# Two-layer sparse-attention trunk on one core: sums moved from GpSimd to VectorE, earlier rotary angles, modulation finished inside the dot products, and a fourth buffer with fewer fp32 blocks in the lead-in

## The chip, the cores and the metric

The kernel runs on one core of a Trainium2 chip. Its engines work side by side, each through its own instruction queue in order: TensorE (PE in the profile; PEld is its weight load), VectorE (DVE), ScalarE (ACT), GpSimd (POOL), and SyncE (SP), which here only issues DMA transfers. Sixteen DMA engines move data between HBM and the on-chip memory. The metric is the device time of one execution in microseconds (us).

## The reference, cut to what matters

Two layers over a sequence of 256 tokens of width 1024, in fp32. Each layer has a mixing and a feed-forward half:

```python
ada = silu(c) @ w_ada[l] + b_ada[l]               # c is one vector; 6 x 1024 results
sh_m, sc_m, g_m, sh_f, sc_f, g_f = split(ada, 6)
h = rms_norm(x, norm_mix[l]) * (1.0 + sc_m) + sh_m
q_a, kc_a, vc_a, ..., g_br = split(h @ w_in[l], ...)  # 4888 columns
y_a = nsa_mixer(...)      # 8 heads of 64: compressed blocks, selected blocks, window
y_b = moba_mixer(...)     # 8 heads of 64
gate_a, gate_b = split(sigmoid(g_br), 2)
x = x + g_m * ((gate_a * (y_a @ w_up_nsa[l]) + gate_b * (y_b @ w_up_moba[l])) @ w_out[l])
h = rms_norm(x, norm_ffn[l]) * (1.0 + sc_f) + sh_f
gt, up = split(h @ w_ffn_in[l], 2)
x = x + g_f * ((silu(gt) * up) @ w_ffn_out[l])
```

Queries and keys are RMS-normalised per head and rotated: `x1*cos - x2*sin`, `x2*cos + x1*sin`, with angles position times 32 inverse frequencies.

## The kernel before

**Who sets the order.** The function `trunk_kernel` describes the work as operations on named values that live in numbered slots of a few arenas. A planner (`Program.order`, `replay` and `rounds`) then decides when the kernel is built in which order every engine issues its operations. It knows one cost for every operation (`_vec`, `act`, `mm` and the figures handed to `raw`), ranks operations by the length of the chain behind them plus a boost, and keeps the best of 60 rounds. Operations allowed on several engines (`engs=("DVE", "POOL")`) are placed by it as well. So a changed cost, slot or engine changes the order of the whole program. For PE there is a constant `STICK`, a bonus for an operation whose array form is that of the one before; it is 0, so unused. A "form" other than `FLAT` is a matmul that uses 64 or fewer rows or columns of the array.

**Dense products.** A weight unit of 128 x 2048 values is loaded into a slot of arena `raw` and split into two fp32r parts by `split_unit`: ACT copies `hi`, DVE subtracts to get `lo`. `mm3` then issues three matmuls per tile (hi*hi, hi*lo, lo*hi). The slot of `raw` is free again when `lo` has been computed. Weights in the tuple `WHOLE` are not split; they are multiplied as plain fp32, and their slot is free only when PE has read it for the last time. An fp32 matmul appears in the profile as two instructions.

**Lead-in (`lead_in`, layer 0).** The normalised x is transposed, and for each of eight blocks k of 128 rows of `w_in` the kernel loads 1 MB of `w_ada` into a slot of `sa` and 1816 columns of `w_in` into a slot of `raw` (three slots; a fourth, 11, only serves values marked spare). Two dot products on DVE (`ada_dot`, one SCALAR_TENSOR_TENSOR of 128x1024 with accumulator each) give shift and scale of the block; `ada_mod` adds the bias and multiplies by the norm's gain in two small DVE operations (`mod_m`); ACT forms the modulated block `hd`, splits it into `hp`, and PE multiplies it into eight PSUM banks. The blocks 0, 2, 4 and 6 are in `WHOLE`.

The table of rotary angles (`angles`) and the products with the gains (`rope_tables`, tiles `ct` and `st`) are computed on POOL; the inverse frequencies come from the array `rows`, loaded after the weights of blocks 0 and 1. The tables of layer 1 are written into the same tiles as soon as layer 0 no longer reads them.

**After the lead-in**, `post_grpA`, `post_qa` and `post_qb` normalise and rotate heads (`rstd_of` does its power -0.5 on POOL; the sums of the two rotated halves may go to DVE or POOL), `mlp` computes the compressed keys and values, and the dense products of the other columns of `w_in`, attention (`nsa`, `moba`), up projections, output projection and feed-forward follow. The remaining `w_ada` rows are streamed through three `aw` tiles and dotted on DVE between other work.

Of the kernel before, what the change touches and what calls it, by code (L numbers as in the profile page):

```python
# [139 lines left out]
class Program:  # L140
# [10 lines left out]
    FLAT, STICK = (P, P), 0.0  # L151
# [417 lines left out]
class Engines:  # L569
# [22 lines left out]
    def tt(self, out, a, b, op, engs=("DVE",)):  # L592
        self._vec(engs, cols(out), True, lambda v: v.tensor_tensor(AP(out), AP(a), AP(b), op=op), [a, b], [out])  # L593
# [9 lines left out]
    def ttr(self, out, a, b, op0, op1, init, accum):  # L603
        self._vec(("DVE",), cols(out), True,
                  lambda v: v.tensor_tensor_reduce(AP(out), AP(a), AP(b), 1.0, init, op0, op1, AP(accum)),  # L605
                  [a, b], [out, accum])
# [114 lines left out]
def trunk_kernel(tc, pools, A):  # L721
# [240 lines left out]
    def rstd_of(ss, n, mul, add, tag):  # L962
# [3 lines left out]
        E_.raw("POOL", 1.1 + 0.13 * n, lambda: nc.gpsimd.tensor_tensor(AP(r), AP(r), AP(mh), op=ALU.pow), [r, mhalf], [r])  # L966
        return r

    def h_rstd(t, log):
# [16 lines left out]
        else:  # L986
            ts(r, s1, 1.0 / D, b, ALU.mult, ALU.add)
            E_.raw("POOL", 1.0, lambda: nc.gpsimd.tensor_tensor(AP(r), AP(r), AP(mhalf), op=ALU.pow), [r, mhalf], [r])
        return xr, r

    def log_soon(late):

        R.boost = 1000.0
        op = R.op({"ACT": (1.28, [lambda: nc.scalar.preload_act_table_set("natural_log_exp_and_others")])}, late, [])
        op.loads = TABLES[3]
        R.boost = 0.0

# [148 lines left out]
    def lead_in(bs, h, W):  # L1146
# [671 lines left out]
```

## Time and profile before

| | us |
|---|---|
| runs shown | 806.29, 2772.15, 805.36 |
| median of them | 806.29 |
| profiled execution, its time | 805.06 |
| span inside the profiled execution | 803.3 |

The profile's page gives busy time per engine, the span in 40 slices, the chain of work that ended last, and groups of instructions by line. Other views are the windows (busy time of each engine in stretches of the span), the timeline (merged instructions in order of time: start, duration, engine, line, operation, and in brackets the idle time before it and what ended it) and the waits. PE's matmuls are pipelined, so a matmul's duration is longer than its distance from the next one; what one costs is read from long unbroken stretches. The TensorE clock was granted in full (9 in every slice, 1.00 in the windows).

### The profile page before, as it was taken

Reading aid. Unit: us, or ns where it says so; the run is one execution under the profiler, and the core shown is the slowest. Engines: PE = TensorE matmul, PEld = TensorE weight load, DVE = VectorE, ACT = ScalarE, POOL = GpSimd, SP = SyncE. Lnnn points to the kernel's source line nnn. Section 1 sums busy time; section 2 is a strip of 40 time slices with the busy share of each in tenths; the row PEclk is TensorE's granted clock in tenths of the full one; section 3 lists DMA queues with packets and bytes.
Section 4 is the critical chain, followed back from the end, with each engine's and each line's share of the span. In section 5 each row is a group of like instructions: output and inputs, shape, how many; then the busy total and the mean of one; then the engine's idle time right before and its main releaser. Section 6 shows DMA issues by size and latency. Waiting matters only on the chain.

```text
span 803.3 us, 10733 instructions
## 1 busy us (share of the span) xinstructions
PE 787.8 (98%) x4062; PEld 623.5 (78%) x4062; DVE 601.1 (75%) x1034; ACT 436.0 (54%) x688; POOL 75.3 (9%) x73
## 2 busy tenths in 40 slices
PE   8998999999999999999999999999999999999997
PEld 4566676778788888888888777677888888888886
DVE  6879999999797878776798799977758435536445
ACT  5445587976373344533585457796538343444432
POOL 3813600001000000000000331000010000000000
PEclk9999999999999999999999999999999999999999
DMA  9967754788758887977774785526573536546631
GB/s 359 415 243 264 253 199 156 239 282 313 267 184 339 317 304 260 337 288 248 301 258 154 271 290 172 191 73 202 198 255 93 170 105 224 191 162 210 209 105 53
DMA packets 74116, 183.85 MB, mean 229 GB/s; under 512 B 4304, under 2 KB 9808, under 8 KB 73552
## 3 DMA queue, kind: packets, MB, share of 16 engines
q1 hardware_dynamic: 73920, 183.08, 64.1%
q8 instruction: 32, 0.52, 0.3%
q14 instruction: 20, 0.16, 0.1%
q10 hardware_dynamic: 144, 0.08, 0.0%
HBM read 182.10 MB, written 1.05 MB: 228 GB/s over the span
## 4 chain that ended last, share of the span: by engine, by line
PE 67%; DVE 5%; ACT 1%; issue 1%; DVEq 0%; ACTq 0%
PE bank L678 61%; PE bank L685 4%; PE bank L659 2%; DVE lo L593 2%; DVE tmp L593 1%; ACT at L642 1%; DVE ss L620 0%; DVE x L593 0%; DVE aw L599 0%; ACT hi L642 0%; DVE at L605 0%; DVE e L593 0%; ACT hp L642 0%; DVE mT L599 0%; DVE tmp L599 0%
## 5 line engine op out<-in xcount | busy, mean ns | idle before, releaser
L678 PE MATMUL bank<-hi,hp 128*128 128x512 f32 (+2 forms) x1344 | 375.6, 383 | 1.6 <-ACT hp L642 0.9
L593 DVE TENSOR_TENSOR lo<-raw,hi 128x2048 fp32r<-128x2048 f32 (+2 forms) x118 | 268.8, 2295 | 121.7 <-ACT hi L642 120.2
L642 ACT ACTIVATE hi<-raw 128x2048 fp32r<-128x2048 f32 (+2 forms) x118 | 221.3, 1893 | 211.8 <-PE bank L678 189.8
L678 PEld LDWEIGHTS bank<-hi,hp 128*128 128x128 f32 x1344 | 243.2, 188 | 56.6 <-issue 6.0
L678 PE MATMUL bank<-lo,hp 128*128 128x512 f32 (+2 forms) x672 | 219.8, 382 | 0.3 <-DVE lo L593 0.3
L678 PEld LDWEIGHTS bank<-lo,hp 128*128 128x128 f32 x672 | 123.8, 188 | 24.8 <-DVE lo L593 2.1
L678 PE MATMUL bank<-hi,aT 128*128 128x512 f32 x352 | 100.4, 394 | 0.3 <-ACT aT L642 0.3
L599 DVE SCALAR_TENSOR_TENSOR aw<-aw,crow 128x1024 f32<-128x1024 f32 x80 | 96.5, 1229 | 4.2 <-DMA aw<-in_w_ada 4.2
L678 PEld LDWEIGHTS bank<-hi,aT 128*128 128x128 f32 x352 | 65.0, 188 | 13.8 <-ACT hi L642 0.6
L678 PE MATMUL bank<-lo,aT 128*128 128x512 f32 x176 | 56.7, 392 | 0.0
L678 PE MATMUL bank<-hi,mT 128*128 128x512 f32 x128 | 40.8, 396 | 0.8 <-DVE mT L599 0.8
L678 PE MATMUL bank<-hi,yy 128*128 128x512 f32 x128 | 40.2, 396 | 0.0
L685 PE MATMUL bank<-ident,tmp 128*128 128x128 f32 x256 | 37.3, 275 | 2.8 <-DVE e L593 0.7
L685 PEld LDWEIGHTS bank<-ident,tmp 128*128 128x128 f32 x256 | 29.9, 140 | 11.5 <-ACT e L651 1.8
L678 PEld LDWEIGHTS bank<-lo,aT 128*128 128x128 f32 x176 | 32.7, 188 | 6.7
L642 ACT ACTIVATE at<-at,nb,rqa 128x128 f32<-128x128 f32 (+1 forms) x64 | 34.1, 535 | 0.7 <-DVE nb L599 0.6
L605 DVE CUSTOM_DVE_ANT_0 at<-bank,maskf 128x128 f32<-128x128 f32 (+1 forms) x96 | 30.6, 351 | 1.6 <-PE bank L685 1.2
L642 ACT ACTIVATE tmp<-bank 128x512 f32<-128x512 f32 (+2 forms) x43 | 20.8, 513 | 18.2 <-PE bank L678 7.2
L593 POOL TENSOR_TENSOR tmp<-tmp,tmp 128x512 f32<-128x512 f32 (+2 forms) x12 | 13.7, 1139 | 176.4 <-DVE tmp L599 158.1
L678 PEld LDWEIGHTS bank<-hi,yy 128*128 128x128 f32 x128 | 24.0, 188 | 6.0 <-issue 0.5
L678 PEld LDWEIGHTS bank<-hi,mT 128*128 128x128 f32 x128 | 23.8, 188 | 6.1 <-DVE mT L599 1.6
L593 DVE TENSOR_TENSOR tmp<-tmp,bank 128x512 f32<-128x512 f32 (+1 forms) x24 | 15.3, 639 | 15.3 <-PE bank L678 14.8
(184 smaller groups left out, 769.9 us busy)
## 6 DMA issues: line engine op xcount, KB each, us to landing
raw<-in_w_ffn_in SPq DMA_DIRECT2D x44, 1024.0 KB, 6.3
aw<-in_w_ada SPq DMA_DIRECT2D x80, 512.0 KB, 5.9
raw<-in_w_in SPq DMA_DIRECT2D x30, 1024.0 KB, 5.2
raw<-in_w_ffn_out SPq DMA_DIRECT2D x22, 1024.0 KB, 5.0
raw<-in_w_out SPq DMA_DIRECT2D x8, 1024.0 KB, 5.1
raw<-in_w_in SPq DMA_DIRECT2D x8, 908.0 KB, 9.2
sa<-in_w_ada SPq DMA_DIRECT2D x7, 1024.0 KB, 12.3
raw<-in_w_up_nsa SPq DMA_DIRECT2D x4, 1024.0 KB, 5.1
```

Of the source, the lines that this page charges most:

```text
L593: self._vec(engs, cols(out), True, lambda v: v.tensor_tensor(AP(out), AP(a), AP(b), op=op), [a, b], [out])
L599: lambda v: v.scalar_tensor_tensor(AP(out), AP(a), AP(s), AP(b), op0=op0, op1=op1, **{k: AP(x) for k, x in kw.items()}),
L605: lambda v: v.tensor_tensor_reduce(AP(out), AP(a), AP(b), 1.0, init, op0, op1, AP(accum)),
L642: op = self.p.op({"ACT": (c, [lambda: self.nc.scalar.activation(AP(out), AP(a), func, **{k: AP(x) for k, x in kw.items()})])}, reads + lis ...
L659: op = self.p.op({"PE": (cost, [lambda: self.nc.tensor.matmul(AP(out), AP(lhsT), AP(rhs), start=start, stop=stop)])}, [lhsT, rhs], [out])
L678: self.nc.tensor.matmul(AP(out), AP(lhsT), AP(rhs), start=first, stop=v.gone == v.terms)
L685: op = self.p.op({"PE": (0.109, [lambda: self.nc.tensor.transpose(AP(out), AP(a), AP(ident))])}, [a, ident], [out])
```

## The change

- **Sums.** The sums of rotated halves, of the queries and of the two gated branches, which could go to DVE or POOL, are DVE only.
- **Angles.** The inverse frequencies move from `rows` to `vecs`, which arrives first. A ScalarE table set with Silu, Sin and Tanh is loaded at the start. Layer 1's `rope_tables` must wait for the gate tile of layer 0's feed-forward.
- **Modulation.** `ada_dot` becomes one `tensor_tensor_reduce` whose scale is a column of the (halved) norm gains and whose start value is a column of the bias prepared by `ada_ready`; `ada_mod` and the bias sums go.
- **Lead-in.** Its raw blocks have an arena of their own, `lraw`, with slots 0, 1, 2 and 17; `WHOLE` is `(0, 3)`.
- **Planner.** `STICK` is 20 and applies after a form that is not `FLAT`, to any other such form; some costs are set anew.

```diff
+SETS = ("exp_and_others", "trig_and_small", "silu_and_others", "natural_log_exp_and_others")
...
-    FLAT, STICK = (P, P), 0.0
+    FLAT, STICK = (P, P), 20.0
...
-                    if e == "PE" and self.STICK:
+                    if e == "PE" and self.STICK and form != self.FLAT:
                         pick = max((c for c in cs if c[0] <= t0 + w), key=lambda c: (
-                            c[1].rank(e) + (self.STICK if c[1].forms and c[1].forms[0] == form else 0.0), -c[1].no))
+                            c[1].rank(e) + (self.STICK if c[1].forms and c[1].forms[0] != self.FLAT else 0.0), -c[1].no))
...
-    def ttr(self, out, a, b, op0, op1, init, accum):
+    def ttr(self, out, a, b, op0, op1, init, accum, scale=1.0):
         self._vec(("DVE",), cols(out), True,
-                  lambda v: v.tensor_tensor_reduce(AP(out), AP(a), AP(b), 1.0, init, op0, op1, AP(accum)),
-                  [a, b], [out, accum])
+                  lambda v: v.tensor_tensor_reduce(AP(out), AP(a), AP(b), AP(scale), AP(init), op0, op1, AP(accum)),
+                  [a, b, init, scale], [out, accum])
...
-WHOLE = (0, 2, 4, 6)
+WHOLE = (0, 3)
...
     arena("raw", (0, 1, 2, 11), (11,))
+    arena("lraw", (0, 1, 2, 17))
...
-    inv = rows.of("inv")[:, :32]
+    inv = vecs.of("inv")[:, NV + 3:NV + 35]
...
-    def ada_dot(w, col):
-        stt(w, w, 0.5, crow, ALU.mult, ALU.mult, accum=col)
-
-    def ada_mod(l, k0, ks, part=None):
-        v = mods[l][k0].of(part)
-        tt(v[:, :, ks], v[:, :, ks], bT[:, l, k0:k0 + 2, ks], ALU.add)
-        tt(v[:, 1, ks], v[:, 1, ks], normT[:, k0 // 3, l, ks], ALU.mult)
+    def ada_dot(w, l, kind, k, col):
+        by = normT[:, kind // 3, l, k:k + 1] if kind in (1, 4) else 0.5
+        ttr(w, w, crow, ALU.mult, ALU.add, bT[:, l, kind, k:k + 1], col, by)
+
+    def ada_ready():
+        ts(normT, normT, 0.5, None, ALU.mult)
+        for a, kind in enumerate((1, 4)):
+            b, nv = bT[:, :, kind], normT[:, a]
+            stt(b, b, 1.0, nv, ALU.add, ALU.mult)
+            ts(b, b, 2.0, None, ALU.mult)
...
-        E_.raw("POOL", 1.1 + 0.13 * n, lambda: nc.gpsimd.tensor_tensor(AP(r), AP(r), AP(mh), op=ALU.pow), [r, mhalf], [r])
+        E_.raw("POOL", 0.5 + 0.22 * n, lambda: nc.gpsimd.tensor_tensor(AP(r), AP(r), AP(mh), op=ALU.pow), [r, mhalf], [r])
...
-            raws[k] = R.val("raw", lambda a: a[:, :NC0])
+            raws[k] = R.val("lraw", lambda a: a[:, :NC0])
...
         dma(vecs, A["vecs"], q="ACT")
+        table_soon(2, [])
...
-        for kind in (1, 4):
-            ts(bT[:, :, kind], bT[:, :, kind], 1.0, None, ALU.add)
+        ada_ready()
...
-                tt(kk.of(br)[:, br * 128:(br + 1) * 128], a, c, ALU.add, engs=("DVE", "POOL"))
+                tt(kk.of(br)[:, br * 128:(br + 1) * 128], a, c, ALU.add)
...
-                    tt(dst, src, pe, ALU.add)
+                    tt(dst, src, pe, ALU.add, extra=0.08)
...
-                    mm(s[:, p * 64:(p + 1) * 64], q[:, p], kbd, False, p == 3)
+                    mm(s[:, p * 64:(p + 1) * 64], q[:, p], kbd, False, p == 3, cost=0.2)
...
-            rope_tables(l, gvec[l])
+            rope_tables(l, gvec[l], [ada[l - 1]["g_f"]])
```

More of the change, by code (lines that the diff above doesn't have):

```diff
@@ L590, in _vec, with tt @@
         self.p.op(alts, reads, writes)
-    def tt(self, out, a, b, op, engs=("DVE",)):
-        self._vec(engs, cols(out), True, lambda v: v.tensor_tensor(AP(out), AP(a), AP(b), op=op), [a, b], [out])
+    def tt(self, out, a, b, op, engs=("DVE",), late=(), extra=0.0):
+        self._vec(engs, cols(out), True, lambda v: v.tensor_tensor(AP(out), AP(a), AP(b), op=op),
+                  [a, b, *late], [out], extra=extra)
     def stt(self, out, a, s, b, op0, op1, accum=None):
@@ L803, in trunk_kernel @@
     NV = 2 * L * KD + L * 6 * KD + L * 16
-    vecs = const("vecs", [P, NV + 3])
-    rows = const("rows", [P, 32 + 256 * L])
+    vecs = const("vecs", [P, NV + 35])
+    rows = const("rows", [P, 256 * L])
     posi = vecs.of("pos")[:, NV:NV + 3].bitcast(I32)
-    inv = rows.of("inv")[:, :32]
-    gvec = [rows.of("g")[:, 32 + 256 * l:32 + 256 * (l + 1)] for l in range(L)]
+    inv = vecs.of("inv")[:, NV + 3:NV + 35]
+    gvec = [rows.of("g")[:, 256 * l:256 * (l + 1)] for l in range(L)]
     normT = vecs.of("norm")[:, :2 * L * KD].rearrange("p (a l k) -> p a l k", a=2, l=L)
@@ L987, in h_rstd, with table_soon @@
             ts(r, s1, 1.0 / D, b, ALU.mult, ALU.add)
-            E_.raw("POOL", 1.0, lambda: nc.gpsimd.tensor_tensor(AP(r), AP(r), AP(mhalf), op=ALU.pow), [r, mhalf], [r])
+            E_.raw("POOL", 0.75, lambda: nc.gpsimd.tensor_tensor(AP(r), AP(r), AP(mhalf), op=ALU.pow), [r, mhalf], [r])
         return xr, r
+    def table_soon(i, late):
+        R.boost = 1000.0
+        op = R.op({"ACT": (1.28, [lambda: nc.scalar.preload_act_table_set(SETS[i])])}, late, [])
+        op.loads = TABLES[i]
+        R.boost = 0.0
     def log_soon(late):
[L993 to L996, printed above, removed]
+        table_soon(3, late)
     def h_norm(t, log=True):
@@ L1067, in rope_tables @@
             tt(ct[:np_].rearrange("p a (h d) -> p (a h) d", h=2), g8,
-               sincos[:np_, 0, t, None, :].to_broadcast([np_, 2 * na, 32]), ALU.mult, engs=("POOL",))
+               sincos[:np_, 0, t, None, :].to_broadcast([np_, 2 * na, 32]), ALU.mult, engs=("POOL",), late=late)
             tt(st[:np_].rearrange("p a (h d) -> p a h d", h=2), gs,
-               nsin[:np_, t, None, :, :].to_broadcast([np_, na, 2, 32]), ALU.mult, engs=("POOL",))
+               nsin[:np_, t, None, :, :].to_broadcast([np_, na, 2, 32]), ALU.mult, engs=("POOL",), late=late)
             CT[t], ST[t] = ct, st
@@ L1303, in post_qa @@
             tt(q.rearrange("p (c g d) -> p g c d", c=4, g=2), a.rearrange("p (g c d) -> p g c d", g=2, c=4),
-               c.rearrange("p (g c d) -> p g c d", g=2, c=4), ALU.add, engs=("DVE", "POOL"))
+               c.rearrange("p (g c d) -> p g c d", g=2, c=4), ALU.add)
             qaT[t] = heads_T(quarter(qv, t, t), q)
@@ L1311, in post_qb @@
             rqb[t] = rstd_of(ss, 8, 1.0, DH * EPS, "rqb")
-            tt(a, a, c, ALU.add, engs=("DVE", "POOL"))
+            tt(a, a, c, ALU.add)
             qbT[t] = heads_T(quarter(qv, 2 + t, 2 + t), a)
@@ L1319, in post_kb @@
             r = rstd_of(ss, 8, 1.0 / DH, EPS, "rkb")
-            tt(a, a, c, ALU.add, engs=("DVE", "POOL"))
+            tt(a, a, c, ALU.add)
             tt(v3(a, DH), v3(a, DH), r[:, :, None].to_broadcast([P, 8, DH]), ALU.mult)
@@ L1411, in mlp @@
             ts(r[:64], ss[:64], 1.0 / DH, EPS, ALU.mult, ALU.add)
-            E_.raw("POOL", 1.2, lambda: nc.gpsimd.tensor_tensor(AP(r)[:64], AP(r)[:64], AP(mhalf)[:64], op=ALU.pow),
+            E_.raw("POOL", 1.5, lambda: nc.gpsimd.tensor_tensor(AP(r)[:64], AP(r)[:64], AP(mhalf)[:64], op=ALU.pow),
                    [r, mhalf], [r])
@@ L1637, in sublayer_mix @@
                 stt(m2, tg[(2 + c, t)], 1.0, bs[("w_up_moba", t)], ALU.add, ALU.mult)
-                tt(m1, m1, m2, ALU.add, engs=("DVE", "POOL"))
+                tt(m1, m1, m2, ALU.add)
                 mT[t] += split_into(quarter(mv[t], 2 * c, c, 0), quarter(mv[t], 2 * c + 1, c, 1), trans4(m1), 0.5)
@@ L1801 @@
                             ("nsa_q_gain", "nsa_k_gain", "moba_q_gain", "moba_k_gain")], axis=1)
-    rows = np.concatenate([np.array(INV_FREQ, np.float32), gains.reshape(-1)])
-    host["vecs"] = np.concatenate([host["vecs"], spots.view(np.float32)], axis=1)
-    host["rows"] = np.repeat(rows[None], P, axis=0)
+    freq = np.repeat(np.array(INV_FREQ, np.float32)[None], P, axis=0)
+    host["vecs"] = np.concatenate([host["vecs"], spots.view(np.float32), freq], axis=1)
+    host["rows"] = np.repeat(gains.reshape(1, -1), P, axis=0)
     arrays, aps = {}, {}
```

9 lines of the change are left out of this document (3 added, 6 removed).

## The prediction

> **What bounds the kernel now.** I read the head of the page, then the windows by stage.
>
> ```profile
> span 803.3 us, 10733 instructions
> PE 787.8 (98%) x4062; PEld 623.5 (78%) x4062; DVE 601.1 (75%) x1034; ACT 436.0 (54%) x688; POOL 75.3 (9%) x73
> ```
>
> ```profile
> 11.74:57.14 45.40, 43.77 (x153) 26.84 (x153) 34.09 (x61) 20.11 (x35) 20.65 (x24) 1.00 0.88 348
> 57.14:70.00 12.86, 9.44 (x103) 7.34 (x104) 12.63 (x30) 6.73 (x15) 2.65 (x2) 1.00 0.61 204
> 70.00:100.00 30.00, 28.28 (x134) 21.37 (x132) 28.45 (x44) 16.22 (x25) 18.46 (x12) 1.00 0.82 285
> 100.00:165.00 65.00, 64.91 (x410) 48.41 (x410) 62.34 (x210) 55.50 (x144) 3.28 (x4) 1.00 0.58 202
> 165.00:440.00 275.00, 273.58 (x1343) 226.30 (x1342) 221.62 (x280) 140.68 (x169) 5.84 (x4) 1.00 0.76 278
> ...
> 790.00:803.30 13.30, 8.65 (x44) 6.61 (x42) 6.53 (x13) 1.75 (x4) 0.00 (x0) 1.00 0.22 80
> ```
>
> The columns are the stretch, its length, busy time of PE, PEld, DVE, ACT and POOL, the granted clock, DMA share and GB/s. PE is the bound: 787.8 of 803.3 us. All its idle time is 15.5 us. So no cover taken off another engine is worth anything except where PE idles: 1.63 us in the lead-in (11.74 to 57.14), 3.42 us behind it (to 70), 1.72 us up to 100, 1.42 us between 165 and 440, and 4.65 us at the end, which this change leaves alone. Everything else must come from fewer PE cycles. Two per cent, about what a measurement of this kernel can tell from no change, is 16 us: more than all the idle time.
>
> **The lead-in: two blocks less in fp32.** Costs of one block are read from the timeline and, for fp32r, from the longest unbroken stretch in the chain.
>
> ```profile
> 23.80 6.27 PE L678 MATMUL bank<-raw,hd 128*128 128x512 f32 x16
> ...
> 231.89 68.46 PE bank L678 x301
> ```
>
> An fp32 block is 16 instructions, 6.27 us. In the chain an fp32r matmul of 512 columns costs 68.46 / 301 = 0.227 us, or 0.444 ns a column. A split block has 3 parts x 2 token tiles x 1816 columns = 10,896 columns: 4.84 us. Two blocks changed from fp32 to split save 2 x 1.43 = 2.9 us; the last fp32 matmul's tail lies inside the 6.27, so I take **2.8 us**, off PE itself. What it adds is two ACT copies and two DVE subtractions:
>
> ```profile
> L593 DVE TENSOR_TENSOR lo<-raw,hi 128x1816 fp32r<-128x1816 f32 x4 | 8.2, 2048 | 3.3 <-ACT hi L642 3.3
> L593 DVE TENSOR_TENSOR mod_m<-mod_m,vecs 128x2 f32<-128x2 f32 (+1 forms) x16 | 3.7, 228 | 0.6
> L593 DVE TENSOR_TENSOR hp<-hd,hp 128x256 fp32r<-128x256 f32 x8 | 4.2, 519 | 2.6 <-ACT hp L642 2.6
> L599 DVE SCALAR_TENSOR_TENSOR aw<-aw,crow 128x1024 f32<-128x1024 f32 x80 | 96.5, 1229 | 4.2 <-DMA aw<-in_w_ada 4.2
> ```
>
> The subtractions cost 2 x 2.05 = 4.1 us, and the sixteen `mod_m` operations that go are worth 3.7. DVE's load in the lead-in stays at about 34.5 of 45.4 us. A split block needs two dots, its `hp` and its `lo`: 2 x 1.23 + 0.52 + 2.05 = 5.03 us of DVE against 4.84 of PE. From block 4 on, with four split blocks in a row, the two run neck and neck; that is a rival below. A block's `hd` follows its dots 2 x 0.23 us sooner.
>
> ```profile
> 18.73 1.56 PE L678 MATMUL bank<-hi,hp 128*128 128x512 f32 x6 [0.63 <-ACT hp L642]
> ...
> 36.23 5.50 PE L678 MATMUL bank<-raw,hd 128*128 128x512 f32 x14 [0.71 <-ACT hd L642]
> ```
>
> These two waits, 1.34 of the stage's 1.63 us, stand behind the dots and `mod_m`; I take **0.4 us** off them, bounds 1.6 gained and 1.5 lost.
>
> **The fourth slot, and what comes after.** The releases explain the loads.
>
> ```profile
> 41.68 0.33 SPq L695 DMA_DIRECT2D raw<-in_w_in  x1
> 46.38 0.33 SPq L695 DMA_DIRECT2D raw<-in_nsa_cmp_k_w  x1
> 46.48 1.72 ACT L642 ACTIVATE hi<-raw 128x1816 fp32r<-128x1816 f32 x1 [0.72 <-DMA raw<-in_w_in]
> ...
> 54.96 1.02 PE L678 MATMUL bank<-raw,hd 128*128 128x512 f32 x2
> 56.01 0.38 SPq L695 DMA_DIRECT2D raw<-in_w_in  x1
> ```
>
> The last raw block was issued at 41.68, when a slot came free, and landed at 46.48. The first weights of the next dense stage were issued at 56.01, just after fp32 block 6 left PE (54.96 + 1.02). With four slots and blocks 4 to 7 split, a slot returns at its subtraction: the lead's queue is never held, and that dense load goes out some 8 us earlier, behind the last lead load and the two `nsa_cmp` loads. What it meets:
>
> ```profile
> 54.93 1.28 ACT L642 ACT_TABLE_LOAD   x1
> 57.78 0.65 PE L685 MATMUL bank<-ident,tmp 128*128 128x128 f32 x4 [0.65 <-ACT e L651]
> 61.95 0.44 PE L685 MATMUL bank<-ident,tmp 128*128 128x128 f32 x2 [0.70 <-DVE e L593]
> 63.70 1.98 PE L659 MATMUL bank<-raw,e 128*31 128x128 f32 x64 [1.26 <-DVE e L593]
> 66.64 2.27 DVE L593 TENSOR_TENSOR lo<-raw,hi 128x2048 fp32r<-128x2048 f32 x1
> ```
>
> PE idles here because only the chain of `post_grpA` feeds it: the first dense unit's `lo` comes at 66.64. Copied and subtracted before 57, it would fill these holes, as soon as the accumulator banks are read out. The early table set also takes the table load (1.28 us) from ACT's path to the first hole. The ScalarE: Activation LUTs page of the Trainium skill (What ACT_TABLE_LOAD costs) puts a switch at about 2.66 us, a load and a drain; here ACT goes on 1.28 us after the load began, so no drain is seen and the sum keeps 1.28. Of 3.42 us idle I take **2.4 us** back; bounds 0 and 3.4. What is late next is DVE, 12.63 of 12.86 busy.
>
> **POOL leaves DVE alone.** Between 70 and 100 DVE is 28.45 of 30 busy, partly because POOL slows it.
>
> ```profile
> 73.92 1.29 POOL L593 TENSOR_TENSOR tmp<-tmp,tmp 128x512 f32<-128x512 f32 x1 [1.60 <-DVE tmp L593]
> 74.36 3.00 DVE L593 TENSOR_TENSOR lo<-raw,hi 128x2048 fp32r<-128x2048 f32 x1
> ...
> 91.54 1.36 DVE L593 TENSOR_TENSOR tmp<-tmp,tmp 32x64 f32<-32x64 f32 x2
> 91.59 0.76 POOL L593 TENSOR_TENSOR st<-rows,nsin 128x256 f32<-128x256 f32 x1 [0.72 <-DVE tmp L593]
> 93.22 0.27 PE L685 MATMUL bank<-ident,kbd_tok 64*128 64x64 f32 x1 [1.41 <-DVE kbd_tok L611]
> ```
>
> The subtraction beside POOL's sum takes 3.00 us, that at 66.64 (quoted above) 2.27: 0.73 lost, and on DVE the sum costs 0.72 (its group, quoted next). So the sum itself is free, and its result is there 0.6 us sooner. The layer-1 tables, which now wait, overlapped the two `tmp` operations (1.36) in the chain for which PE waited 1.41 us. The new wait of the tables holds up POOL's queue only, which the windows show with 3.28 us of work from 100 to 165 and 5.84 from there to 440: little stands behind it. But POOL's power operations stay in the chain of `kbd_tok`. I take **0.5 us** of the 1.72; bounds 1.7 gained, 1.5 lost if the sums only lengthen DVE's queue. The GPSIMD Engine Reference of the Trainium skill (8. Key points) says that POOL shares its memory interfaces with VectorE and that instructions with two on-chip inputs contend; the 3.00 against 2.27 agrees. By the same rule the angles, moved ahead, disturb the dots of the first blocks; that is part of the first rival. The other place where a sum touched PE:
>
> ```profile
> 202.84 1.29 POOL L593 TENSOR_TENSOR tmp<-tmp,tmp 128x512 f32<-128x512 f32 x1 [4.57 <-DVE tmp L599]
> 206.93 0.50 PE L678 MATMUL bank<-hi,mT 128*128 128x512 f32 x1 [0.77 <-DVE mT L599]
> L593 DVE TENSOR_TENSOR tmp<-tmp,tmp 128x512 f32<-128x512 f32 x13 | 9.4, 720 | 0.1
> ```
>
> A DVE sum is 0.72 us instead of 1.29 and spares the subtraction beside it: **0.4 us** of 0.77; bounds 0 and 0.77. The remaining sums lie under a full PE and cost nothing there.
>
> **Early angles.** They ran on POOL deep in the lead-in, behind the load of `rows`.
>
> ```profile
> 7.99 0.74 POOL L988 TENSOR_TENSOR rx<-rx,mhalf 128x1 f32<-128x1 f32 x1 [0.99 <-DVE rx L611]
> ...
> 24.97 1.23 POOL L593 TENSOR_TENSOR tmp<-tmp,tmp 128x96 f32<-128x96 f32 x1
> ```
>
> Now they stand in POOL's queue around the two `rx` (the second is quoted), for which the first transposes wait, and each lasts up to 1.23 us. `ada_ready` adds three small DVE operations before the first dot (0.7 us at the 228 ns of `mod_m`), and the first `mod_m` pair (0.46) goes. Start of block 0: **0.2 us later**; bounds 0.4 earlier and 1.5 later.
>
> **Modulation elsewhere.** The new reduce is seen only on PSUM input with constants.
>
> ```profile
> L605 DVE CUSTOM_DVE_ANT_0 at<-bank,maskf 128x256 f32<-128x256 f32 x48 | 19.0, 417 | 1.4 <-PE bank L685 1.0 <-ACT hi L642 0.5
> L605 DVE CUSTOM_DVE_ANT_0 at<-bank,maskf 128x128 f32<-128x128 f32 x48 | 11.6, 285 | 0.2 <-PE bank L685 0.2
> ```
>
> 128 columns more cost 132 ns, 1.03 ns a column, so 1024 columns take 0.417 + 768 x 0.00103 = 1.21 us against 1.229: nothing. Bounds: 0.1 us less, or half speed, 1.07 us more. **0.**
>
> **Turns of the array.**
>
> ```profile
> 135.05 1.13 PE L659 MATMUL bank<-kk,qq 64*128 64x512 f32 x4
> 136.11 1.09 PE L659 MATMUL bank<-pt,vsw 128*64 128x128 f32 x16
> ```
>
> A burst in another form takes 1.06 us from start to start, where its columns at 0.444 ns (four times 512, two passes each, the two row halves side by side) need 0.91: some 0.15 us a turn. If `STICK` joins two or three bursts: **0.3 us** gained, bounds 1.5 gained (ten joined) and 0.5 lost. The other cost figures only reorder.
>
> **The sum.** 2.8 + 0.4 + 2.4 + 0.5 + 0.4 + 0.3 - 0.2 = 6.6 us. Against the profiled execution: span 803.3 - 6.6 = 796.7, with the 1.8 us around it (805.06 - 803.3) 798.5 us. Of the runs shown the lowest is 805.36 and the median 806.29, so I stay with the profiled execution and keep a microsecond of doubt upward.
>
> **The rivals.**
> - *DVE gives it back* (803.5 us). Six split blocks and the contention of early angles make DVE the clock of the lead-in, the stage behind it, already 98% DVE, gains nothing, and only the saved passes remain, less four blocks at 5.03 instead of 4.84 (0.8) and 0.4 for a later start: 805.06 - 2.8 + 1.2 = 803.5. For: the windows from 57 to 165 show DVE at 95% and more. Against: 11.3 us of DVE idle time in the lead-in. Angles in front of both `rx`, a start 1.5 us late, give 798.5 + 1.3 = 799.8 by themselves, inside the forecast.
> - *The reduce is slower* (814 us, slower than before). If, with two on-chip inputs and column operands, it runs at half speed, each of 16 dots in the lead-in costs 1.07 more: 17 us, of which 11.3 find idle DVE, so 6 remain; and of the 13 between 100 and 165, 14 us, less 2.66 of idle DVE there, 11 remain: 798.5 + 17 = 815, some of it taken up by reordering: 814. It decides from 2.66 / 13 = 0.2 us a dot. For: nothing shows it with column operands. Against: 1.03 ns a column on PSUM.
> - *The plan finds more* (793.4 us): all 6.8 us of idle time from 11.74 to 100 go (3.3 are taken above), the hole at 206 closes (0.4 more) and ten bursts join (1.2 more): 5.1 us under the forecast.
> - *The change doesn't do what it says*, in that the dense load stays behind because the DMA queue, not the slot, held it: then the 2.4 us behind the lead-in are not won, 800.9 us, still in the forecast. Against: 56.01 follows PE's last read at 55.98.
>
> **How the numbers follow.** Forecast, 796 to 801.5: 0.56. DVE gives it back, 801.5 to 805.5: 0.22. More is found, under 796: 0.13. Slower reduce or a worse plan, over 805.5: 0.09. The range reaches into both neighbours: 795 to 804.5. Faster by over 2% means under 790.2, which needs more than all idle time up to 100 beside the passes: 0.02. Slower by over 2%, over 822.4, only if the reduce costs more than half speed: 0.03. The rest, 0.95, is within 2%.
>
> **What would show it.** Right: 32 `raw,hd` matmuls instead of 64; the lead-in's end near 54.5; the first dense `lo` before 57; no table load near 55; no `tmp` sums and, from 70 to 100, no tables on POOL; PE idle from 57 to 70 near 1 us. Wrong: PE waits for `lo` or `hp` in blocks 4 to 7; dots above 1.4 us; new holes of PE after 100, where the plan was full.

## The result, and the profile after

| | before | changed |
|---|---|---|
| median of 8 runs each, us | 806.87 | 801.90 |
| lowest and highest of them | 805.13, 2772.15 (next 809.72) | 800.14, 802.61 |
| profiled execution: time, span | 805.06, 803.3 | 801.24, 799.5 |

The ratio is 0.9938, with a 95% interval of 0.9919 to 0.9956: a small gain, within 2%. The forecast was 798.5 us, with a range of 795 to 804.5.

The head of the changed kernel's page:

```profile
span 799.5 us, 10734 instructions
PE 784.7 (98%) x4077; PEld 626.7 (78%) x4077; DVE 606.7 (76%) x1021; ACT 435.5 (54%) x681; POOL 66.8 (8%) x65
```

and its windows in the stretches used before (columns as there):

```profile
11.74:57.14 45.40, 42.67 (x176) 30.28 (x176) 37.57 (x57) 22.98 (x41) 18.00 (x20) 1.00 0.96 381
57.14:70.00 12.86, 11.45 (x113) 8.99 (x115) 12.70 (x28) 6.52 (x10) 3.04 (x2) 1.00 0.47 170
70.00:100.00 30.00, 27.36 (x136) 21.49 (x135) 27.20 (x54) 15.53 (x28) 14.95 (x6) 1.00 0.76 262
100.00:165.00 65.00, 64.25 (x411) 47.25 (x409) 62.61 (x200) 56.23 (x139) 5.88 (x7) 1.00 0.61 212
165.00:440.00 275.00, 274.15 (x1336) 227.30 (x1335) 225.90 (x276) 139.26 (x167) 1.03 (x1) 1.00 0.76 274
```

PE is busy 3.1 us less (787.8 to 784.7) and idle 0.7 us less (15.5 to 14.8): together the 3.8 us between the spans (the medians lie 5.0 apart; the profiled execution before was one of its faster ones). Idle time of PE by stage is length less busy time:

| stretch | before | changed | difference |
|---|---|---|---|
| 11.74 to 57.14 | 1.63 | 2.73 | +1.10 |
| 57.14 to 70 | 3.42 | 1.41 | -2.01 |
| 70 to 100 | 1.72 | 2.64 | +0.92 |
| 100 to 165 | 0.09 | 0.75 | +0.66 |
| 165 to 440 | 1.42 | 0.85 | -0.57 |

So the time came almost whole from PE's busy time. Behind the lead-in idle time went nearly as forecast; in the lead-in and from 70 to 165 it grew. In these five stretches together it is 0.1 us more, and the 0.7 us less come from the rest of the span. Where it stands, from PE's timeline (start, duration, instruction, and in brackets the idle time before it and who ended it):

```profile
19.18 2.38 PE L680 MATMUL bank<-hi,hp 128*128 128x512 f32 x10 [1.01 <-ACT hi L644]
30.64 5.50 PE L680 MATMUL bank<-lraw,hd 128*128 128x512 f32 x14 [0.77 <-ACT hd L644]
60.34 2.79 PE L680 MATMUL bank<-hi,hp 128*128 128x512 f32 x11 [0.90 <-ACT hi L644]
93.80 0.27 PE L687 MATMUL bank<-ident,kbd_tok 64*128 64x64 f32 x1 [2.31 <-DVE kbd_tok L613]
157.03 0.63 PE L687 MATMUL bank<-ident,at 128*128 128x128 f32 x4 [0.65 <-DVE at L1456]
```

The longest hole is the one before `kbd_tok`, 2.31 us, where it was 1.41. POOL's timeline ahead of it, and DVE's:

```profile
76.73 4.68 POOL L970 TENSOR_TENSOR rqa<-rqa,mhalf 128x8 f32<-128x8 f32 x1 [6.58 <-DVE rqa L613]
81.38 6.37 POOL L970 TENSOR_TENSOR rqb<-rqb,mhalf 128x8 f32<-128x8 f32 x1
87.71 1.63 POOL L970 TENSOR_TENSOR rkb<-rkb,mhalf 128x8 f32<-128x8 f32 x1
89.31 0.54 POOL L1418 TENSOR_TENSOR rc<-rc,mhalf 64x1 f32<-64x1 f32 x1
...
89.38 0.69 DVE L594 TENSOR_TENSOR tmp<-tmp,rkb 128x512 f32<-128x512 f32 x1 [2.53 <-POOL rkb L970]
91.19 2.29 DVE L594 TENSOR_TENSOR lo<-raw,hi 128x2048 fp32r<-128x2048 f32 x1
93.50 0.24 DVE L613 TENSOR_SCALAR kbd_tok<-tmp,rc 32x64 f32<-32x64 f32 x1
```

The same operation, a power on 128x8 values, takes 1.63 us at 87.71 and 6.37 us at 81.38. The power `rc`, from which `kbd_tok` is made, stands behind `rqa`, `rqb` and `rkb` in POOL's queue; DVE waits 2.53 us for `rkb`, and a subtraction comes between the two halves of `kbd_tok`.

### The profile page after: what moved, and what is told of

Its sections match the earlier page's. It is cut to its first block, busy times and chain, and to the rows that moved or that the text cites. A ratio compares the mean times of both kernels' runs of the same rounds, so it can differ in the third digit from the quotient of the medians.

```text
span 799.5 us, 10734 instructions
## 1 busy us (share of the span) xinstructions
PE 784.7 (98%) x4077; PEld 626.7 (78%) x4077; DVE 606.7 (76%) x1021; ACT 435.5 (54%) x681; POOL 66.8 (8%) x65
## 4 chain that ended last, share of the span: by engine, by line
PE 86%; DVE 7%; DMA 3%; POOL 2%; ACT 1%; issue 1%; SPq 0%; DVEq 0%; ACTq 0%
PE bank L680 75%; PE bank L687 5%; PE bank L661 5%; DVE tmp L594 2%; DVE lo L594 2%; DMA sa<-in_w_ada 1%; DVE sa L607 1%; POOL rqb L970 1%; DMA aw<-in_w_ada 1%; DMA raw<-in_w_up_moba 1%; POOL rqa L970 1%; ACT hi L644 0%; DVE e L594 0%; DVE ss L622 0%; SPq L697 0%
## 5 line engine op out<-in xcount | busy, mean ns | idle before, releaser
L680 PE MATMUL bank<-hi,hp 128*128 128x512 f32 (+2 forms) x1376 | 382.7, 382 | 3.1 <-ACT hi L644 1.9
L594 DVE TENSOR_TENSOR lo<-raw,hi 128x2048 fp32r<-128x2048 f32 (+1 forms) x114 | 256.8, 2270 | 110.3 <-ACT hi L644 108.9
L644 ACT ACTIVATE hi<-raw 128x2048 fp32r<-128x2048 f32 (+1 forms) x114 | 214.1, 1899 | 209.9 <-PE bank L680 191.0
L680 PEld LDWEIGHTS bank<-hi,hp 128*128 128x128 f32 x1376 | 248.5, 188 | 59.0 <-ACT hi L644 5.3
L680 PE MATMUL bank<-lo,hp 128*128 128x512 f32 (+2 forms) x688 | 224.4, 381 | 0.0
L680 PEld LDWEIGHTS bank<-lo,hp 128*128 128x128 f32 x688 | 126.6, 188 | 24.7 <-issue 1.1
L607 DVE CUSTOM_DVE_ANT_0 aw<-aw,crow,vecs 128x1024 f32<-128x1024 f32 x80 | 102.1, 1297 | 9.2 <-DMA aw<-in_w_ada 9.0
L970 POOL TENSOR_TENSOR r<-r,mhalf 128x4 f32<-128x4 f32 x4 | 4.2, 1054 | 336.6 <-DVE r L613 336.6
L644 ACT ACTIVATE tmp<-bank 128x512 f32<-128x512 f32 (+2 forms) x43 | 20.8, 513 | 18.5 <-PE bank L687 7.7
```

The lines of the kernel that those rows point to most:

```text
L607: lambda v: v.tensor_tensor_reduce(AP(out), AP(a), AP(b), AP(scale), AP(init), op0, op1, AP(accum)),
L644: op = self.p.op({"ACT": (c, [lambda: self.nc.scalar.activation(AP(out), AP(a), func, **{k: AP(x) for k, x in kw.items()})])}, reads + lis ...
L680: self.nc.tensor.matmul(AP(out), AP(lhsT), AP(rhs), start=first, stop=v.gone == v.terms)
L970: E_.raw("POOL", 0.5 + 0.22 * n, lambda: nc.gpsimd.tensor_tensor(AP(r), AP(r), AP(mh), op=ALU.pow), [r, mhalf], [r])
```

## The experiments

The reading after these traces was that the edits count for less than where the plan sets POOL's operations. In the expectations A is that the saved passes alone pay, B that all parts pay and the new reduce takes some back, C that the plan and POOL's holes decide, D that the edits themselves decide. E is C narrowed down; E, F and G are told where they appear. Ratios are to the kernel before, run on the same chip; its median was 806.2 to 806.9 us on the chips used, so medians from different chips compare to some 0.7 us. The changed kernel's own ratio is 0.9938 [0.9919, 0.9956]. Span and busy time are those of one profiled execution each.

| kernel | median us | ratio [95% interval] | span us, PE busy us |
|---|---|---|---|
| before, planned anew | 808.42 | 1.0024 [1.0013, 1.0035] | 806.6, 788.1 |
| before, lead-in alone | 813.15 | 1.0075 [1.0062, 1.0089] | 811.1, 789.9 |
| before, sums alone | 804.16 | 0.9976 [0.9966, 0.9987] | 801.6, 786.8 |
| changed, planned anew | 802.89 | 0.9945 [0.9932, 0.9957] | 801.3, 786.4 |
| changed, four fp32 blocks | 802.80 | 0.9946 [0.9933, 0.9958] | 801.2, 786.4 |
| changed, old modulation | 802.07 | 0.9942 [0.9930, 0.9955] | 800.0, 785.0 |
| changed, old turn rule | 802.40 | 0.9958 [0.9946, 0.9970] | 798.7, 785.5 |
| changed, sums on POOL too | 810.36 | 1.0041 [1.0025, 1.0057] | 809.3, 788.8 |
| the same, no scaling on POOL | 804.78 | 0.9981 [0.9970, 0.9992] | 802.1, 785.8 |
| changed, tables of layer 1 free | 803.38 | 0.9963 [0.9948, 0.9978] | 801.6, 786.1 |
| changed, no early table set | 799.00 | 0.9911 [0.9898, 0.9924] | 797.2, 784.5 |
| the same, late angles | 798.27 | 0.9890 [0.9870, 0.9910] | 795.4, 784.2 |

**Planning anew.** `RUNS` is a setting of the planner's search alone; nothing is computed differently.

```diff
-    ROUNDS, RUNS, WEIGHT, FADE, START = 60, 8, 2.0, 0.95, 15.0
+    ROUNDS, RUNS, WEIGHT, FADE, START = 60, 7, 2.0, 0.95, 15.0
```

On the changed kernel:

> The changed kernel with the same operations and costs, planned with 7 instead of 8 random replays a round, which gives another order. It shows how far an order alone moves the time: both theories expect the changed kernel's time within 1.5 us (ratio to before 0.992 to 0.996). If it moves by more, single differences of 1 or 2 us between the other kernels say nothing.

and on the kernel before:

> The kernel before, same operations and costs, planned with 7 instead of 8 random replays a round. Theory C (much of the difference is which order the planner happens to find; POOL operations that stand beside long DVE subtractions open holes in PE by chance): differs from the kernel before by 2 to 8 us (ratio outside 0.998 to 1.002). Theory D (the edits themselves make the gain, the order is worth a microsecond as in the changed kernel): ratio 0.998 to 1.002.

The kernel before became 2.2 us slower, and PE idles 18.5 us instead of 15.5, with holes that the kernel before has elsewhere or not at all:

```profile
96.54 0.27 PE L685 MATMUL bank<-ident,kbd_tok 64*128 64x64 f32 x1 [1.63 <-DVE kbd_tok L611]
169.24 0.44 PE L685 MATMUL bank<-ident,at 128*128 128x128 f32 x2 [1.51 <-POOL at L1455]
```

The interval, 1.0013 to 1.0035, reaches a little into what D allows (1.002). So a difference of 2 us between two versions may be the plan's alone. The changed kernel gave nearly the same plan again: POOL's order is the same throughout, and that of PE's first 1323 matmuls. So this run says little on what another order would do to it. Its interval and the changed kernel's overlap; why its profiled span is still 1.8 us longer is told in the last section.

**The lead-in alone**, on the kernel before:

```diff
-WHOLE = (0, 2, 4, 6)
+WHOLE = (0, 3)
+    arena("lraw", (0, 1, 2, 17))
-            raws[k] = R.val("raw", lambda a: a[:, :NC0])
+            raws[k] = R.val("lraw", lambda a: a[:, :NC0])
```

> The kernel before with the lead-in's part alone: blocks 0 and 3 in fp32 and the arena lraw with slots 0, 1, 2 and 17; modulation, sums, angles and planner as before. Theory A (only the saved PE passes pay, the idle time of the stage behind the lead-in stays because its chain over DVE and POOL sets it): 2.8 us faster than before, ratio 0.9965, PE busy about 785, PE idle up to 100 us still near 8.7. Theory B (the parts pay as forecast, and the longer reduce, 1.30 instead of 1.23 us a dot, takes it away again in the changed kernel): 5 to 6 us faster, since this one has no such reduce, ratio 0.993, PE idle up to 100 us near 6.

It is slower, by 6.4 us at the median. The rows, from the timelines of PE, ACT, POOL and DVE:

```profile
32.21 6.73 PE L678 MATMUL bank<-lraw,hd 128*128 128x512 f32 x12 [2.53 <-ACT hd L642]
172.96 0.69 PE L685 MATMUL bank<-ident,at 128*128 128x128 f32 x2 [4.17 <-POOL at L1456]
...
30.39 0.28 ACT L642 ACTIVATE sincos<-tmp 128x96 f32<-128x96 f32 x1 [4.84 <-POOL tmp L611]
165.95 6.96 POOL L1456 TENSOR_SCALAR at<-at,ri 128x256 f32<-128x256 f32 x2 [28.61 <-PE bank L678]
167.96 4.68 DVE L593 TENSOR_TENSOR lo<-raw,hi 128x2048 fp32r<-128x2048 f32 x2
```

ACT's queue stood 4.84 us at a sine that waited for POOL's angles, and `hd` of block 3 behind it. Far from the edit, the new plan gave the softmax's scaling to POOL beside two subtractions: two instructions in 6.96 us, and PE idle for 4.17. These holes, 6.7 us, are more than the passes save. Behind each the TensorE clock was granted at half for 3.41 us, which costs some 3.4 us more (last section). Without that PE's busy time is about 786.5, 1.3 us less than before, so the passes pay here too, but less than 2.8.

**Four fp32 blocks again**, on the changed kernel:

```diff
-WHOLE = (0, 3)
+WHOLE = (0, 2, 4, 6)
```

> The changed kernel with blocks 0, 2, 4 and 6 in fp32 again. Theory A: 2.8 us slower than the changed kernel (ratio to before about 0.9973), so nearly the whole gain is gone. Theory B: 4 us or more slower, since the early dense load goes too (ratio about 0.999).

Busy time of PE rises by 1.7 us (786.4 against 784.7) and the median by 0.9, with overlapping intervals. So A falls: it expected 2.8 us, nearly the whole gain, and the passes are no more than a part of it.

**The old modulation**, `ada_dot` as one SCALAR_TENSOR_TENSOR and `ada_mod` behind it:

```diff
-        ttr(w, w, crow, ALU.mult, ALU.add, bT[:, l, kind, k:k + 1], col, by)
+        stt(w, w, 0.5, crow, ALU.mult, ALU.mult, accum=col)
...
+                ada_mod(0, 0, slice(k, k + 1), part=k)
```

> The changed kernel with the old dots (SCALAR_TENSOR_TENSOR, 1.23 us) and the two small sums and products of ada_mod back. Theory A: within 1 us of the changed kernel (ratio to before 0.994), PE idle up to 100 us near 8. Theory B: 1.5 to 3 us faster than the changed kernel (ratio 0.991), DVE busy 5 us lower and PE idle up to 100 us near 6.

No difference. The groups of the dots, of this kernel and then of the changed one (count, busy time, mean ns, idle time before):

```profile
L601 DVE SCALAR_TENSOR_TENSOR aw<-aw,crow 128x1024 f32<-128x1024 f32 x80 | 96.5, 1226 | 5.9 <-DMA aw<-in_w_ada 5.9
```

```profile
L607 DVE CUSTOM_DVE_ANT_0 aw<-aw,crow,vecs 128x1024 f32<-128x1024 f32 x80 | 102.1, 1297 | 9.2 <-DMA aw<-in_w_ada 9.0
```

A dot costs 71 ns more and 5.6 us in all on DVE, and the time does not show it. B, which expected 1.5 to 3 us, falls with that.

**The old turn rule:**

```diff
-    FLAT, STICK = (P, P), 20.0
+    FLAT, STICK = (P, P), 0.0
```

> The changed kernel with the planner's turn rule as before (STICK 0). By the prediction's term (turns, 0.3 us) 802.2 us; theory E: 800 to 806 us, set by what the new plan does with GpSimd's operations, with the busy time of PE within 0.5 us of 784.7 at an undisturbed clock.

802.4 against 801.9, with overlapping intervals: the rule is worth no more than this can tell. The busy time, 785.5, is 0.8 above the changed kernel's, where 0.5 was the most expected. The profiled execution is the fastest of the six (800.45, the others 801.97 to 803.66), so its span is no sign of a gain.

**Sums on POOL again**, in five places of the changed kernel, like this one:

```diff
-            tt(a, a, c, ALU.add)
+            tt(a, a, c, ALU.add, engs=("DVE", "POOL"))
```

> The changed kernel with the sums again allowed on DVE or POOL. Theory D with the sums as the source: 2 us or more slower than the changed kernel (ratio to before 0.997 or more), with a new PE wait behind a POOL tmp. Forecast's working (0.4 + 0.2 us): within 1 us of the changed kernel (0.994 to 0.9955).

It loses 8.5 us, more than the whole gain. But the two largest holes have no sum in them (PE's timeline, POOL's, DVE's):

```profile
166.17 0.69 PE L687 MATMUL bank<-ident,at 128*128 128x128 f32 x2 [1.87 <-POOL at L1461]
168.65 0.69 PE L687 MATMUL bank<-ident,at 128*128 128x128 f32 x2 [1.79 <-POOL at L1461]
...
162.64 5.96 POOL L1461 TENSOR_SCALAR at<-at,ri 128x256 f32<-128x256 f32 x2 [38.26 <-DVE ri L626]
163.56 4.69 DVE L594 TENSOR_TENSOR lo<-raw,hi 128x2048 fp32r<-128x2048 f32 x2
```

It is the softmax's scaling again, 5.96 us for two instructions beside two subtractions. From 166.09 to 172.92 us the clock was granted at half; PE was busy for 4.96 us of that, so about 2.5 us more are lost. Hence theory E: what counts is which POOL operation the plan sets beside VectorE's long subtractions; against it F: the sums themselves cost.

**The same without scaling on POOL**, where only DVE and ACT may scale:

```diff
-            alts["POOL"] = (nh * (0.46 + nk * 1.0e-3),
-                            [(lambda i: lambda: nc.gpsimd.tensor_scalar(AP(p3)[:, i], AP(p3)[:, i], AP(ri)[:, i:i + 1], 0.0,
-                                                                        op0=ALU.mult, op1=ALU.add))(i) for i in range(nh)])
```

> The changed kernel with the sums allowed on GpSimd again, and the softmax's scaling by 1/sum not allowed there. Theory E: the 8.5 us that the sums cost were two scalings that ran 2.4 to 3.5 us each beside subtractions at 163 to 169 us, with the lower clock behind them; without them 800 to 804 us. Theory F: the sums cost it themselves, 808 to 811 us.

5.6 of the 8.5 us went with the scaling; 2.9 stayed, a little more than E allowed (804 us). Part of them shows in the windows, with 1.40 us more idle time of PE from 165 to 440 and 0.88 more from 440 to 490 than the changed kernel has (0.85, above, and 50 less 49.79). Other stretches made up 0.8 of that, and PE's busy time is 1.1 us longer:

```profile
165.00:440.00 275.00, 272.75 (x1325) 225.06 (x1325) 227.45 (x274) 136.68 (x163) 14.04 (x10) 1.00 0.76 275
440.00:490.00 50.00, 48.91 (x299) 38.05 (x298) 45.55 (x105) 29.22 (x56) 21.76 (x10) 1.00 0.79 271
```

**The sums alone**, the same edit the other way round, on the kernel before:

```diff
-            tt(a, a, c, ALU.add, engs=("DVE", "POOL"))
+            tt(a, a, c, ALU.add)
```

> The kernel before with one thing alone changed: the five sums may run on VectorE only. Theory E (no edit by itself, but where the plan sets GpSimd operations beside VectorE's long subtractions): the sums were at most 15 us of GpSimd work and held PE once (0.77 us at 206.93), so 804 to 808 us, and any larger difference shows as a PE hole behind a GpSimd operation that is not a sum. Theory F (the sums themselves cost the 8.5 us that putting them back into the changed kernel cost): 798 to 801 us.

2.2 us faster, the fast end of E's range, and far from F's 798 to 801: the one part that gained by itself. But planning this kernel anew moved it by as much the other way, so how much of the 2.2 is the sums' own is not shown; that both directions (2.2 here, 2.9 above) agree speaks for them. The windows, where before had 9.44 and 28.28:

```profile
57.14:70.00 12.86, 9.90 (x105) 7.51 (x105) 12.18 (x29) 6.28 (x14) 1.08 (x1) 1.00 0.60 206
70.00:100.00 30.00, 28.78 (x144) 22.68 (x142) 28.86 (x45) 17.15 (x28) 17.01 (x12) 1.00 0.85 299
```

PE's busy time, 786.8, is 1.0 us lower although no matmul was taken away, as it was 1.1 us higher with the sums put back; what makes it so is not settled.

**The tables of layer 1 free again:**

```diff
-            rope_tables(l, gvec[l], [ada[l - 1]["g_f"]])
+            rope_tables(l, gvec[l])
```

> The changed kernel without the wait of layer 1's tables for the feed-forward gate, so that POOL computes them between 75 and 110 us again. Theory D with the tables as the source: 2 us or more slower than the changed kernel. Forecast's working (part of 0.5 us): within 1 us (ratio to before 0.994 to 0.9955).

1.5 us slower at the median (the intervals just overlap). POOL's timeline, and PE's:

```profile
82.50 5.47 POOL L594 TENSOR_TENSOR ct<-rows,sincos 128x256 f32<-128x256 f32 x1
...
95.42 0.27 PE L687 MATMUL bank<-ident,kbd_tok 64*128 64x64 f32 x1 [2.98 <-DVE kbd_tok L613]
```

A table in front of the powers `rkb` and `rc` takes 5.47 us (a like one 0.73, last section), and the hole before `kbd_tok` is 2.98 us. Behind it the clock was at half for 3.41 us, some 1.7 us lost, which is all the busy time that this version has more (786.1 against 784.7).

**No early table set, with late angles and without:** the first version has the angles behind the rows again and no early set, the second only leaves out the set.

```diff
-        table_soon(2, [])
...
-        tt(a3, posf[:, :, None].to_broadcast([P, 3, 32]), inv[:, None, :].to_broadcast([P, 3, 32]), ALU.mult, engs=po)
+        tt(a3, posf[:, :, None].to_broadcast([P, 3, 32]), inv[:, None, :].to_broadcast([P, 3, 32]), ALU.mult, engs=po, late=[rows])
```

> The changed kernel with the angles made to wait for the array rows again and without the early table set, so that POOL computes angles beside the split blocks and ACT's sine waits for them. If the lead-in of the kernel with the lead-in's part alone lost its time to the angles in ACT's queue (a 2.5 us hole before hd of block 3), this one shows the same hole and is 2 to 4 us slower than the changed kernel (ratio to before 0.997 to 0.999). If early angles are worth nothing: within 1 us (0.994 to 0.9955).

> The changed kernel without the early load of the sine's table set; the angles stay free of the rows. Theory E: what the version with late angles gained was the order of GpSimd's powers at 80 to 94 us (PE wait 2.31 us there); so about 798 us if rc's power runs ahead of the four others here too, and 801 to 803 us if it is again behind them, whatever the lead-in does. Theory G (the early table set itself costs, in the lead-in): 798 us in both cases, with PE idle before 57 us lower by 2 us or more.

They are 3.6 and 2.9 us faster than the changed kernel, and the first, at 798.27 us, is the fastest version measured. Its interval lies clear of the changed kernel's; that of the second just overlaps it. Late angles were expected to cost 2 to 4 us or nothing, so neither case came, and early angles show no gain. G (the early set costs in the lead-in) falls: without it PE is busy 8.67 + 43.54 = 52.21 us up to 57, against 52.90 with it, so it idles more there, not less. The gain lies from 70 to 100, where E put it, and 0.7 us more from 100 to 165. In the version without the set:

```profile
0.00:10.00 10.00, 8.67 (x30) 4.16 (x30) 6.32 (x23) 4.41 (x9) 4.27 (x17) 1.00 0.83 303
10.00:57.00 47.00, 43.54 (x188) 31.19 (x189) 38.38 (x58) 25.89 (x40) 18.11 (x24) 1.00 0.93 373
70.00:100.00 30.00, 29.89 (x149) 23.52 (x149) 29.86 (x60) 17.69 (x28) 11.86 (x6) 1.00 0.83 289
```

and POOL's timeline of the same version:

```profile
81.98 1.06 POOL L1417 TENSOR_TENSOR rc<-rc,mhalf 64x1 f32<-64x1 f32 x1 [10.54 <-DVE rc L613]
83.02 3.33 POOL L970 TENSOR_TENSOR rkb<-rkb,mhalf 128x8 f32<-128x8 f32 x1
88.85 1.67 POOL L970 TENSOR_TENSOR rqa<-rqa,mhalf 128x8 f32<-128x8 f32 x1 [2.50 <-DVE rqa L613]
```

PE idles 0.11 us there instead of 2.64. `rc` is raised first, and `rqa` and `rqb` of the other tile come after it. That these two versions got this order and the changed kernel not is the plan's doing; why a table load in the first microseconds turns it was not traced, and an order of the powers set by hand was not tried.

Two other runs warn against taking this order for the whole cause. With the old turn rule `rc` stands as far back as in the changed kernel, yet the powers there took 1.63, 3.09 and 4.88 us instead of 4.68, 6.37 and 1.63, and the hole is 0.71 us. With the old modulation `rc` was raised early (at 82.73) and there is no such hole, but one of 2.05 at 164.92, behind a scaling on POOL. Neither was faster at the median. What E says of POOL beside VectorE fits all of them; which single hole decides is not shown.

## Why the prediction was right or wrong

The total fell inside the forecast of 796 to 801.5 by its profiled execution (801.24). By the median (801.90) it lies 0.4 us above, in the stretch that was given to "DVE gives it back". Of the 6.6 us of the sum the spans show 3.8. The working held only in part, and that the total came so near is in part luck.

- **Passes, 2.8 us: the right place, somewhat too large.** `lraw,hd` has 32 matmuls instead of 64, and PE's busy time fell by 3.1, but not by the passes alone. From the start of block 0 to the last product of the lead-in PE is busy 46.91 us before, 44.45 in the changed kernel and 46.76 with four fp32 blocks again: 2.3 to 2.5 us. Over the whole span the blocks account for 1.3 us (lead-in alone) and 1.7 (four blocks again), the sums for 1.0, each in a plan of its own. The lead-in's unbroken run of products ends at 56.72 instead of 57.14, not near 54.5.
- **Behind the lead-in, 2.4 us: near (2.01).** There is no table load near 55, and dense products fill the holes. But the first `lo` of a dense unit came at 60.68, not before 57, as SP's, ACT's and DVE's timelines show:

```profile
36.23 0.33 SPq L697 DMA_DIRECT2D lraw<-in_w_in  x1
46.79 1.73 ACT L644 ACTIVATE hi<-lraw 128x1816 fp32r<-128x1816 f32 x1 [1.90 <-DMA lraw<-in_w_in]
48.56 2.04 DVE L594 TENSOR_TENSOR lo<-lraw,hi 128x1816 fp32r<-128x1816 f32 x1
50.63 0.38 SPq L697 DMA_DIRECT2D raw<-in_w_in  x1
...
58.10 0.38 ACT L653 ACTIVATE kk<-bank 128x256 f32<-128x256 f32 x1 [1.60 <-PE bank L687]
58.38 1.91 ACT L644 ACTIVATE hi<-raw 128x2048 fp32r<-128x2048 f32 x1
60.68 2.29 DVE L594 TENSOR_TENSOR lo<-raw,hi 128x2048 fp32r<-128x2048 f32 x1
```

  The step that failed is "the lead's queue is never held". From 36.23 on the loads went out one a block, 4.8 us apart, each 0.03 us after a subtraction had given a slot back (the last at 48.56 + 2.04 = 50.60), and this one 5.4 us earlier than at 56.01, not 8. What set that pace, the text had left out: the DMA engines were full (a share of 1.00 to 1.04 from 10 to 45 us, 409 to 423 GB/s). The copies of blocks 4 to 7 each waited for their data, at 32.40, 37.20, 42.03 and 46.79. So the last block was issued 5.5 us sooner than before (36.23 against 41.68) and landed no sooner (46.79 against 46.48). Then the dense unit's copy stood in ACT's queue behind the read-out of `kk`, which waited 1.60 us for PE.
- **Waits of the lead-in, 0.4 us gained: wrong, 1.10 lost.** The waits of block 1 and block 3 are now 1.01 and 0.77 us, for ACT's `hi` and `hd`. In block 1 ACT made `hi` after `hd` and `hp` (at 17.43); in the kernel before it came ahead of them (16.02). In block 3 `hd` waited 5.22 us for DVE, whose dots took 1.75 us each beside POOL's tables, instead of about 1.3:

```profile
28.19 1.75 DVE L607 CUSTOM_DVE_ANT_0 sa<-sa,crow,vecs 128x1024 f32<-128x1024 f32 x1
27.14 1.72 POOL L594 TENSOR_TENSOR ct<-rows,sincos 128x256 f32<-128x256 f32 x1
28.83 1.70 POOL L594 TENSOR_TENSOR st<-rows,nsin 128x256 f32<-128x256 f32 x1
29.99 0.60 ACT L644 ACTIVATE hd<-pt,mod_m 128x256 f32<-128x256 f32 x1 [5.22 <-DVE mod_m L607]
```

  The 0.46 us that `mod_m` saved a block was lost again there. DVE is busy 9.95 of the 10 us from 20 to 30 (7.07 before), and 37.57 us in the stage, not 34.5. "Dots above 1.4 us", named as a sign against the forecast, came for this one block.
- **70 to 100, 0.5 us gained: wrong, 0.92 lost**, inside its bound of 1.5. No sums and no tables were on POOL there, as said. The text looked at what POOL does to DVE (3.00 us against 2.27) and left out what DVE does to POOL, 6.37 us against 1.63; it named the powers in the chain of `kbd_tok` and did not price their wait.
- **"The remaining sums lie under a full PE and cost nothing there": not borne out.** Putting them back cost 2.9 us, with 2.3 us more idle time from 165 to 490, and removing them from the kernel before won 2.2, where 0.4 + 0.5 were reckoned for the places in sight.
- **The hole at 206.93, 0.4 of 0.77: it went whole.** New holes after 100, named as a sign against the forecast, did come: 0.65 at 157.03.
- **Reduce, 0:** it takes 71 ns more where 20 less were worked out, and the median shows nothing of it. **Turns, 0.3:** too small to tell. **Start of block 0, 0.2 later:** 11.81 against 11.74.

So the idle terms, 3.7 us in all, brought 0.7, and the small error of the total hides errors of 1.5 us in two of them. The rival nearest in time, that the dense load stays behind (800.9), came true only in that the load was 2.6 us later than thought: the 2.4 us it denies were won to 2.01. "DVE gives it back" (803.5) came true in part: DVE beside POOL's early tables was what block 3 waited for. But PE did not wait in blocks 4 to 7, and the stage behind the lead-in did gain. The rest was given back by the order of POOL's and ACT's queues.

## What to carry to other kernels

Where PE is 98% busy, rank what remains by the queue that releases it: a 0.5 us operation on GpSimd can take 3 us or more when the plan sets it beside VectorE's long two-input operations. So keep GpSimd off chains that PE waits for; putting the shortest such chain first in its queue is worth a trial (the two fastest versions have it so, by the plan). Where a planner reorders the whole program, measure a version that is only planned anew before a gain of some 2 us is ascribed to an edit. An edit that helps in one plan can lose in another; test it in both directions, added to the old kernel and taken out of the new one. And where transfers already fill the DMA engines, a load that is issued sooner does not land sooner.

## What the runs showed of the hardware

Of GpSimd and VectorE, one waits for the other, as the rows below show. Beside back-to-back subtractions GpSimd loses far more than VectorE. Two subtractions took 4.69 us at 163.56 in the version with the sums on POOL, 2.35 each instead of 2.27, while the scalings beside them took 2.98 each (5.96 / 2). In the version with the lead-in alone it was 3.48 (6.96 / 2). In the kernel before the scaling takes 0.48, as the view of tile `at` shows (count, then shortest, median and longest in ns):

```profile
L1455 POOL TENSOR_SCALAR at<-at,ri x2: 479/480/481, 144.4 to 144.8; 128x256 f32<-128x256 f32 x2
```

GpSimd does not run slowly there; it waits the subtractions out. Its operation ends when VectorE's run of two-input operations has ended and its own undisturbed time (1.63 us for a power, 0.73 for a table) has passed since, to within 0.13 us. In the changed kernel the powers at 76.73 and 81.38 end at 81.41 and 87.75, and the runs beside them end at 79.91 and 86.24; in the version with the old turn rule it is 81.43 and 87.76 after 79.92 and 86.25, and for the table of 5.47 us in the version with free tables 87.97 after 87.36.

In the other direction VectorE waits. The subtraction of 3.00 us at 74.36, quoted in the prediction, ends 2.15 us after POOL's sum does, and alone it takes 2.27. And in the version with free tables a multiplication by a broadcast column began during the power `rc` (89.53 to 90.07) and ended 0.55 us after the table behind it:

```profile
89.59 1.74 DVE L594 TENSOR_TENSOR tmp<-tmp,rkb 128x512 f32<-128x512 f32 x1 [1.63 <-POOL rkb L970]
90.05 0.73 POOL L594 TENSOR_TENSOR st<-rows,nsin 128x256 f32<-128x256 f32 x1
```

The same multiplication took 0.69 us in the changed kernel (at 89.38). So which of the two pays is not fixed by the engine. What decides a close start is not shown: the power at 76.73 took 4.68 us in the changed kernel and 1.63 us, at 76.74, with the old turn rule, beside the same operations of VectorE.

A hole of PE can cost twice. The window behind the hole of 2.30 us in the version planned anew:

```profile
95.50:99.00 3.50, 3.50 (x17) 2.86 (x15) 3.11 (x6) 0.82 (x3) 0.00 (x0) 0.53 0.92 299
```

The clock was granted at half for 3.41 us there, some 1.7 us lost. Behind the hole of 2.31 us in the changed kernel it was granted in full, 1.00 in the same window. That is most of the 1.8 us between the two spans, from the same plan at that place.

The traces show why like holes differ. In every one of them the clock changes only on a grid of 3.41 us that goes on through the whole span (in the version planned anew at 95.39, 98.80 and 801.95; the last two lie 206 steps of 3.4133 us apart). What counts is PE's idle time within one step of this grid. In the version planned anew 2.13 of the 2.30 us fell into one step, and the next was at half. In the changed kernel the hole was cut into 0.76 and 1.55. Between the first 10 us of the span and the last 15, in all fourteen profiled executions, the six steps with 1.79, 1.87, 2.13, 2.53, 2.83 and 3.41 us of idle time were each followed by a step at half clock, and no step with 1.65 us or less was. So the limit, an estimate from these steps, lies near 1.7 us, half a step. It is not known more sharply: near the end of the version with free tables one step with 1.92 us was not followed by half clock. The hole of 2.05 us in the version with the old modulation was cut too, and left no more than 1.27 in one step.

The page TensorE: Matmul & The Clock Gate of the Trainium skill (What's actually happening) has a free-running window of about 3.4 us: half the clock after an idle one, the full clock after a busy one. The grid agrees with it; how much idle time makes a window an idle one the traces add. Its advice to avoid gaps above some 3 us (Why this matters for your kernels) is too lax here: a hole of 2.30 us was enough, and two of 1.87 and 1.79 us were too.
